# DMA transposes through DRAM for k, q, f, most of v and most head outputs

## The chip, the cores and the metric

The kernel runs on one core of one Trainium2 chip. The metric is the time of one execution in microseconds; lower is better. The core has a matrix engine (PE, with its weight loads shown as PEld), a vector engine (DVE), a scalar engine (ACT), GpSimd (POOL), and SyncE (SP), whose queue here only issues DMAs. ACT can issue DMAs from its own queue too. Sixteen DMA engines carry what these queues issue.

## The reference

Two layers of a decoder trunk over 256 tokens of width 2048, in float32. Each layer normalises h, multiplies it by one wide input matrix (8208 columns), and gives the columns to two groups of heads: group A, eight heads of gated DeltaNet in chunkwise form (short causal conv and SiLU on q, k, v, l2-normed q and k, a triangular inverse), and group B, eight heads of HGRN2 (a gated linear recurrence). Each head's output is RMS-normed and gated, the outputs are joined and multiplied by an output matrix; then a per-layer embedding gated by a sigmoid is added.

```python
for l in range(DEPTH):
    hn = rms_norm(h, norm_w[l])
    proj = hn @ w_in[l]
    dn_qkv, dn_z, dn_b, dn_a, hg_q, hg_f, hg_i, hg_z = jnp.split(proj, split_points, axis=-1)
    y_a = deltanet_branch(dn_qkv, dn_z, dn_b, dn_a, ...)
    y_b = hgrn2_branch(hg_q, hg_f, hg_i, hg_z, lower_bounds[l], hg_norm_w[l])
    h = h + jnp.concatenate([y_a, y_b], axis=-1) @ w_out[l]
    gate = jax.nn.sigmoid(h @ w_ple_gate[l])
    h = h + (p[l] @ w_ple_up[l]) * gate
return rms_norm(h, final_norm_w)
```

## The kernel before, in words

**Dense products.** Weights arrive from DRAM in float32 and are split into two parts whose product PE takes at its fast float32r rate: `whi`, a rounded copy made by ACT (L438), and `wlo`, the remainder made by DVE (L440). Activations are split in the same way (`split`: hi on ACT, lo on DVE). Each product is three matmuls (hi x hi, lo x hi, hi x lo), all recorded at L377. The work of a layer is a list of steps: a step is two row blocks (128 each) of the weights for 512 columns, 12 matmuls; a chunk of columns is 8 such steps. Chunks 0 (z of the first group and the two gate inputs, 272 columns) and 10 (v of the first group alone, 256 columns) take four row blocks in a step. The input stage has 17 chunks in the order of `in_order()`: z and gates, kq of groups 0 to 3, then fq(0), iz(0), fq(1), iz(1), fq(2), v(0), vz(1), iz(2), vz(2), fq(3), vz(3), iz(3). A "group" is two heads. The out stage and the gate stage have four chunks of 512 columns each; the first two chunks of each stage are interleaved.

**Loads.** `ahead(n)` is called before step n: it issues loads (L419, SP's queue, three buffers `raw`) and makes the splits two steps ahead (three buffers `whi` and `wlo`).

**The work between.** All the rest (conv, gates, inverse, states, norms) is written as generators. `spawn` starts one; each `yield n` hands back the number of steps that it wants to wait, and `tick()`, called after each step, advances those whose count has run out. A generator that yields a function waits until that is true. The numbers come from the tables `DELAY` (by kind of work: d DeltaNet, i inverse, b the turning of h, h HGRN2) and `DELAY_AT` (by group or layer, as "d2yp"). PE's order is the program's order; `while not pairs_ready(...)` in the out and gate stages calls `tick()` with no step between when an operand isn't made yet.

**Transposes.** The projection gives tokens on partitions, the mixers want channels on partitions. `evict` copies a chunk from PSUM to SBUF on ACT (tile `et`); `turned` turns it on PE in groups of four 128x128 transposes (L380) into PSUM. This is done for k and q (`dkdq`), f and q of HGRN2 (`hfhq`), v (`dv`, which is turned a second time after conv and SiLU: tile `pv`), and each head output (`head_norm`: tile `yt`, turned into `yp`, then split to `y[kp]`; kp is 0 to 3 for DeltaNet's groups, 4 to 7 for HGRN2's). The out stage takes its row blocks in the order of `OUT_KTS`, so it wants y[4], y[5], y[0], y[1], y[6], y[2], y[3], y[7]:

```python
OUT_KTS = (8, 9, 10, 11, 0, 1, 2, 3, 12, 13, 4, 5, 6, 7, 14, 15)
```

For three of four chunks of h, before the gate stage (g) and before the next layer (n), the turn already goes by DMA (`turn_by_dma`): ACT copies 16-bit halves apart (L548), a DMA transpose on SP's queue goes from SBUF to SBUF (L551), and ACT joins the halves again (L556).

**The inverse.** When the fourth group has given its matrix (`given`, a write to DRAM from ACT's queue, L682), `Inverse.run` makes the triangular inverse of all groups in a chain of DVE and PE work, with DMAs through DRAM. v of a group then goes through pz, pS, pw, pz, po to its output.

Of the kernel before, what the change touches and what calls it, by code (L numbers as in the profile page):

```python
# [8 lines left out]
F32 = mybir.dt.float32  # L9
# [24 lines left out]
def chunk_cols(chunk):  # L34
# [3 lines left out]


DELAY = {  # L40
    "d": {'c': 1, 'D': 4, 'k': 6, 'q': 7, 'ssq': 1, 'v': 5, 'z0': 1, 'S': 1, 'w': 1, 'z1': 1, 'o': 1, 'y': 3, 'yp': 1},
    "i": {'F': 4, 'F2': 1, 'F3': 1, 'F4': 1, 'w': 2, 'b': 1, 'T': 2, 't16': 3, 'p16': 2, 't32': 3, 'p32': 2, 't64': 3, 'p64': 2},
    "b": {'o': 1, 'g': 4},
    "h": {'c': 1, 'f': 1, 'x2': 1, 'x4': 1, 'x8': 1, 'a': 2, 'x16': 1, 'x32': 1, 'x64': 1, 'u16': 2, 'u64': 1, 'o': 2, 'y': 2, 'yp': 1, 'q': 0},
}

DELAY_AT = {
# [14 lines left out]
}  # L62


XB = 1, 1, 4, 1, 1


def delay(kind, g, step):
# [107 lines left out]
def trunk(ctx: ExitStack, tc: tile.TileContext, head, xT, x, pT, W, par, fw, cst, msk, eye, out):  # L176
# [311 lines left out]
    def tmp(name, shape=(128, 512)):  # L488
        return tp.tile([128, 512], F32, tag="tmp", name=name)

    def sigmoid(dst, src, e=None):

        if e is None:
            S.activation(dst, src, AF.Exp, scale=-1.0)
            V.tensor_scalar(dst, dst, BIG, 1.0, ALU.min, ALU.add)
        else:
            S.activation(e, src, AF.Exp, scale=-1.0)
            V.tensor_scalar(e, e, BIG, None, ALU.min)
            V.tensor_scalar(dst, e, 1.0, None, ALU.add)
        S.activation(dst, dst, AF.Ln)  # L500
        S.activation(dst, dst, AF.Exp, scale=-1.0)

# [27 lines left out]
    def turn(c, name, scales):  # L530
# [8 lines left out]
            out.append(split(ps, 2 * c + half, scales(2 * c + half), name))  # L539
        return out  # L540

    def turn_by_dma(c, name, scales):

        u16 = lambda ap: ap.bitcast(U16)
        flat, across = (u16(mix("et", 1024, 2, f"{name}{x}{c}")).rearrange("p (w k m b) -> p w k m b", w=2, k=4, m=2)
                        for x in "pq")
        for m in range(2):
            S.copy(flat[:, :, :, m], u16(h[c][:, m]).rearrange("p (k b w) -> p w k b", k=4, w=2))  # L548
            yield XB[m]
        every = lambda ap: ap.rearrange("p w k m b -> p (w k m) b")  # L550
        nc.sync.dma_start_transpose(every(across), flat.rearrange("p w k m b -> p (w k m b)"))  # L551
        yield XB[2]
        out = []
        for half in range(2):
            t = tmp(f"{name}t{c}{half}")
            S.copy(u16(t).rearrange("p (b w) -> p w b", w=2),  # L556
                   across[:, :, 2 * half:2 * half + 2].rearrange("p w k m b -> p w (k m b)"))
            yield XB[3 + half]
            out.append(split(t, 2 * c + half, scales(2 * c + half), name))
        return out  # L560

    first_ss = []
# [51 lines left out]
    def mix(tag, n, bufs, name):  # L614
        return mp.tile([128, n], F32, tag=tag, name=name, bufs=bufs)
# [4 lines left out]
    def head_norm(o, f, sz, nw, kp, y, name, wait):  # L620

        yt = tmp(name + "yt")
        for i in range(4):
            hh, t = divmod(i, 2)
            V.scalar_tensor_tensor(v4(yt)[:, i], o[:, i], f[:, i:i + 1],
                                   sz[:, 256 * t + 128 * hh:256 * t + 128 * hh + 128], ALU.mult, ALU.mult)
        yield wait
        ps = pm.tile([128, 512], F32, tag="m", name=name + "yp")
        for i in range(4):
            PE.transpose(ps[:, 128 * i:128 * i + 128], v4(yt)[:, i], ident)  # L630
        y[kp] = split(ps, kp, [nw], name)

    def gate_z(ps, c0, rt, name):
# [6 lines left out]
        G.tensor_tensor(sz, zs, sz, ALU.mult)  # L640
        return sz

    def evict(ps, c0, n, rt, name):

        et = mix("et", 1024, 2, name + "et")[:, :2 * n].rearrange("p (t n) -> p t n", t=2)
        for t in range(2):
            S.activation(et[:, t], ps[t][:, c0:c0 + n], AF.Copy, scale=rt[:, t:t + 1])
        return et

    def turned(et, c0, name):  # L650

# [10 lines left out]
    class Inverse:  # L662
# [2 lines left out]
        NT = 4 * NG  # L665

        def __init__(self, l):
            self.n, self.l, self.Bt, self.have, self.ready = f"di{l}", l, None, 0, False

        def wait(self, step):  # L670
            return delay("i", self.l, step)
# [122 lines left out]
    class DN:  # L794
# [41 lines left out]
        def conv(self, ps, which):  # L836
# [11 lines left out]
            sg = tmp(n + "sg")  # L848
            sigmoid(sg, ac)
            return ac, sg  # L850

        def conv_silu_kq(self, ps, which, w):
            ac, sg = self.conv(ps, which)
            for t in range(2):
                V.tensor_tensor(self.kq[t][:, :, w, :], v4(ac)[:, t::2], v4(sg)[:, t::2], ALU.mult)

# [10 lines left out]

        def dkdq(self, ps, c0):
            n = self.n
            et = evict(ps, c0, 512, self.row.rt, n + "kq")  # L870
            yield self.wait("c")
            pk, pq = turned(et, 0, n + "pkc"), turned(et, 256, n + "pqc")
            self.kq = [mix(f"kq{t}", 512, 2 + 2 * t, n + f"kq{t}").rearrange("p (h w c) -> p h w c", h=2, w=2)
                       for t in range(2)]
            self.conv_silu_kq(pk, 1, 0)
            spawn(self.k_side())
            self.conv_silu_kq(pq, 0, 1)
            spawn(self.q_side())

        def k_side(self):  # L880
# [52 lines left out]

        def dv(self, ps, c0):
            n, kq, g = self.n, self.kq, self.g
            et = evict(ps, c0, 256, self.row.rt, n + "v")
            yield self.wait("c")
            ac, sg = self.conv(turned(et, 0, n + "pvc"), 2)
            V.tensor_tensor(ac, ac, sg, ALU.mult)
            yield self.wait("v")  # L940
            yield self.after("b")
            pv = pm.tile([128, 512], F32, tag="m", name=n + "pv")
            for i in range(4):
                PE.transpose(pv[:, 128 * i:128 * i + 128], ac[:, 128 * i:128 * i + 128], ident)
# [35 lines left out]
            po = pm.tile([128, 512], F32, tag="m", name=n + "po")  # L980
            for i in range(4):
                PE.matmul(po[:, 128 * i:128 * i + 128], self.QK[:, i], v1[:, i], start=True, stop=True)
            o = v4(tmp(n + "o"))
            S.copy(o[:, 0::2], v4(po)[:, 0::2])
            V.tensor_tensor(o[:, 1::2], v4(po)[:, 1::2], qs, ALU.add)
# [9 lines left out]
            yield from head_norm(o, f, self.sz, P("dnw", self.l), g, self.y, n, self.wait("yp"))  # L995

    class HG:

# [16 lines left out]
            yield 1  # L1015

        def hfhq(self, ps, c0):
            et = evict(ps, c0, 512, self.row.rt, self.n + "fq")
            yield self.wait("c")
            spawn(self.f_side(turned(et, 0, self.n + "pf")))  # L1020
            spawn(self.q_side(turned(et, 256, self.n + "pq")))

        def f_side(self, fs):
            l, g, n = self.l, self.g, self.n
            e, sg = tmp(n + "fe"), tmp(n + "fsg")
            sigmoid(sg, fs, e)
# [13 lines left out]
        def q_side(self, qr):  # L1040
# [5 lines left out]
            sigmoid(sg, qr)  # L1046
# [133 lines left out]
        def hz(self, ps, c0):  # L1180
            g = self.g
            sz = gate_z(ps, c0, self.row.rt, self.n)
            yield self.wait("y")
            yield self.after("o")
            yield from head_norm(self.o, self.f, sz, P("hnw", self.l), 4 + g, self.y, self.n, self.wait("yp"))


    def banks(name, c):
# [293 lines left out]
```

## Time and profile before

| | |
|---|---|
| Median of 3 runs | 1234.73 us (1233.22 to 1235.4) |
| The profiled execution's own time | 1233.27 us |
| Its span, first to last instruction | 1231.6 us |
| Granted clock of PE | 0.998 |
| Busy: PE, DVE, ACT | 1216.1, 880.9, 807.7 us |
| DMA queue of the loads, share of 16 engines | 54.7% |

"Busy" is the time in which an engine had an instruction under way. The chain that ended last is followed back from the last instruction: at each step to what released it, or to the instruction before it on its engine. A row of a tile's view gives count, the durations (least, median, most, in ns), and when the first and the last started. In a view of waits the numbers are the total in us, how many times, and the longest. Names like dn02pkc are tiles: dn or hg, the layer, the group, the tile.

### The profile page before, as it was taken

Reading aid. Unit: us, or ns where it says so; the run is one execution under the profiler, and the core shown is the slowest. Engines: PE = TensorE matmul, PEld = TensorE weight load, DVE = VectorE, ACT = ScalarE, POOL = GpSimd, SP = SyncE. Lnnn points to the kernel's source line nnn. Section 1 sums busy time; section 2 is a strip of 40 time slices with the busy share of each in tenths; the row PEclk is TensorE's granted clock in tenths of the full one; section 3 lists DMA queues with packets and bytes.
Section 4 is the critical chain, followed back from the end, with each engine's and each line's share of the span. In section 5 each row is a group of like instructions: output and inputs, shape, how many; then the busy total and the mean of one; then the engine's idle time right before and its main releaser. Section 6 shows DMA issues by size and latency. Waiting matters only on the chain.

```text
span 1231.6 us, 21477 instructions
## 1 busy us (share of the span) xinstructions
PE 1216.1 (99%) x8282; PEld 1021.8 (83%) x8282; DVE 880.9 (72%) x1537; ACT 807.7 (66%) x1376; POOL 75.3 (6%) x67
## 2 busy tenths in 40 slices
PE   9999999999999999999999999999999999999997
PEld 8888887898888888888888888878888888888886
DVE  7777897887568756547668879877875696565565
ACT  7676766586757757548866667674857676575453
POOL 0310000000000100000003100000000010000020
PEclk9999999999999999999999999999999999999999
DMA  8555455534464456657665555555444555686564
GB/s 290 177 193 175 159 182 164 188 139 170 156 213 150 171 176 210 219 197 202 222 188 177 180 175 175 174 176 159 132 147 150 175 159 178 199 214 222 180 205 137
DMA packets 92727, 223.42 MB, mean 181 GB/s; under 512 B 34256, under 2 KB 39760, under 8 KB 92624
## 3 DMA queue, kind: packets, MB, share of 16 engines
q1 hardware_dynamic: 82400, 216.65, 54.7%
q10 hardware_dynamic: 10224, 5.39, 1.6%
q8 instruction: 65, 1.06, 0.3%
q14 instruction: 38, 0.31, 0.1%
HBM read 212.84 MB, written 4.46 MB: 176 GB/s over the span
## 4 chain that ended last, share of the span: by engine, by line
PE 93%; ACT 4%; issue 1%; DMA 1%; DVE 1%; POOLq 0%; POOL 0%; ACTq 0%; DVEq 0%
PE out L377 14%; PE gate L377 11%; PE in0hf L377 7%; PE in1hf L377 7%; PE in1dk L377 7%; PE in1hi L377 7%; PE in0hi L377 7%; PE in0dv L377 6%; PE in1dv L377 6%; PE in0dk L377 5%; PE up L377 1%; ACT whi L438 1%; PE in0dz L377 1%; PE in1dz L377 1%; DMA n1q<-n1p 0%
## 5 line engine op out<-in xcount | busy, mean ns | idle before, releaser
L440 DVE TENSOR_TENSOR wlo<-raw,whi 128x1024 fp32r<-128x1024 f32 (+2 forms) x393 | 479.6, 1224 | 278.3 <-ACT whi L438 273.0
L438 ACT ACTIVATE whi<-raw 128x1024 fp32r<-128x1024 f32 (+2 forms) x393 | 408.9, 1045 | 249.6 <-PE gate L377 51.1
L377 PE MATMUL in1hi<-whi,n1hi 128*128 128x512 f32 x128 | 41.0, 402 | 0.0
L377 PE MATMUL in1hf<-whi,n1hi 128*128 128x512 f32 x128 | 40.5, 398 | 0.0
L377 PE MATMUL in1dk<-whi,n1hi 128*128 128x512 f32 x128 | 40.4, 397 | 0.0
L377 PE MATMUL gate<-whi,g0hi 128*128 128x512 f32 x128 | 39.6, 391 | 0.2 <-ACT pg L1236 0.2
L377 PE MATMUL in1hi<-whi,n1lo 128*128 128x512 f32 x128 | 39.7, 391 | 0.0
L377 PE MATMUL in1dk<-whi,n1lo 128*128 128x512 f32 x128 | 39.6, 390 | 0.0
L377 PE MATMUL in1hf<-whi,n1lo 128*128 128x512 f32 x128 | 39.5, 390 | 0.0
L377 PE MATMUL gate<-whi,g0lo 128*128 128x512 f32 x128 | 39.4, 389 | 0.0
L377 PE MATMUL in1dv<-whi,n1hi 128*128 128x512 f32 (+1 forms) x128 | 36.5, 376 | 0.0
L377 PE MATMUL gate<-whi,g1hi 128*128 128x512 f32 (+1 forms) x120 | 35.7, 379 | 0.0
L377 PE MATMUL gate<-whi,g1lo 128*128 128x512 f32 (+1 forms) x120 | 35.7, 379 | 0.0
L377 PE MATMUL in1dk<-wlo,n1hi 128*128 128x512 f32 x128 | 35.6, 390 | 0.0
L377 PE MATMUL in1hi<-wlo,n1hi 128*128 128x512 f32 x128 | 35.6, 390 | 0.0
L377 PE MATMUL in1hf<-wlo,n1hi 128*128 128x512 f32 x128 | 35.6, 389 | 0.0
L377 PE MATMUL gate<-wlo,g0hi 128*128 128x512 f32 x128 | 35.5, 389 | 0.0
L377 PE MATMUL in1dv<-whi,n1lo 128*128 128x512 f32 (+1 forms) x128 | 34.9, 364 | 0.0
L377 PE MATMUL gate<-wlo,g1hi 128*128 128x512 f32 (+1 forms) x120 | 32.4, 379 | 0.0
L377 PE MATMUL in1dv<-wlo,n1hi 128*128 128x512 f32 (+1 forms) x128 | 31.5, 363 | 0.0
L377 PE MATMUL in0hi<-whi,n0hi 128*128 128x512 f32 x96 | 30.8, 402 | 0.0
L377 PE MATMUL in0hf<-whi,n0hi 128*128 128x512 f32 x96 | 30.7, 401 | 0.0
(1491 smaller groups left out, 2917.1 us busy)
## 6 DMA issues: line engine op xcount, KB each, us to landing
raw<-W SPq DMA_DIRECT2D x383, 512.0 KB, 3.6
raw<-W SPq DMA_DIRECT2D x7, 544.0 KB, 3.9
h<-x SPq DMA_DIRECT2D x4, 512.0 KB, 4.9
xt<-xT SPq DMA_DIRECT2D x3, 512.0 KB, 6.6
out_dram<-h SPq DMA_DIRECT2D x5, 256.0 KB, 2.3
di0d<-di0Bt ACTq DMA_DIRECT2D x4, 256.0 KB, 2.4
di1d<-di1Bt ACTq DMA_DIRECT2D x4, 256.0 KB, 2.3
fw<-fw ACTq DMA_DIRECT2D x2, 512.0 KB, 4.0
```

The costliest lines, as they stand in the source:

```text
L377: return tc.keep_in_program_order(nc.tensor.matmul(*a, **k))
L438: S.activation(hi[:, sl], raw[:, sl], AF.Copy)
L440: V.tensor_tensor(lo[:, sl], raw[:, sl], hi[:, sl].bitcast(F32), ALU.subtract)
```

## The change

The transposes of k and q, of f and q (all groups), of v in groups 0 to 2 (both turns), and of head outputs 0, 1, 2, 4, 5 go by DMA. `apart` copies the 16-bit halves of each word apart on ACT, one copy per 128 tokens and a step ahead of each, and writes them to DRAM from ACT's queue. `across` issues a DMA transpose from DRAM to SBUF on SP's queue; since the two halves of a word are neighbouring rows in DRAM, the words come back whole. `turn_by_dma` uses the same two functions, and so loses the copy that joined the halves. The group 3 of v and the outputs 3, 6, 7 stay on PE. The sigmoids are cut into steps (`sigmoid_in_steps`), the conv into taps and SiLU with steps between, and a group of v starts its state steps only when the group before has finished its own (`inv.through`). The distances are set anew.

```diff
-    "d": {'c': 1, 'D': 4, 'k': 6, 'q': 7, 'ssq': 1, 'v': 5, ... 'y': 3, 'yp': 1},
+    "d": {'c': 3, 'D': 4, 'k': 6, 'q': 7, 'ssq': 1, 'v': 5, 'z0': 1, 'S': 1, 'w': 1, 'z1': 1, 'o': 1, 'y': 3, 'yp': 1, 'e': 2, 've': 2, 'vc': 3, 'vp': 1, 'vt': 2, 'vq': 3, 'ye': 2, 'yt': 3, 's': 1, 's1': 1, 's2': 1},
-    "b": {'o': 1, 'g': 4},
+    "b": {'o': 1, 'g': 4, 'e': 2, 't': 3},
-    "h": {'c': 1, ...
+    "h": {'c': 3, ... 'e': 2, 'ye': 2, 'yt': 3, 's2': 1},
...
-    "d1k": 5, "d1ssq": 3, "d1w": 2, "d1y": 4, "d1yp": 2,
-    "d2D": 3, "d2k": 9, "d2o": 4, "d2q": 11, "d2ssq": 4, "d2v": 6, "d2yp": 2,
+    "d1D": 6, "d1c": 5, "d1e": 4, "d1k": 5, "d1ssq": 3, "d1vt": 3, "d1w": 2, "d1y": 2, "d1yp": 2, "d1yt": 4,
+    "d2D": 6, "d2k": 9, "d2o": 4, "d2q": 11, "d2s2": 2, "d2ssq": 4, "d2v": 4, "d2yt": 4,
...
-XB = 1, 1, 4, 1, 1
+V_DMA = 0, 1, 2
+Y_DMA = 0, 1, 2, 4, 5
...
+    def apart(src, name, into=None):
+        n, c = src.shape[1:]
+        for t in range(n):
+            yield 1
+            if not t:
+                flat = (tmp if n * c == 512 else et_tile)(name + "pl") if into is None else into
+                flat = u16(flat).rearrange("p (n w c) -> p n w c", n=n, w=2)
+            S.copy(flat[:, t], u16(src[:, t]).rearrange("p (c w) -> p w c", w=2))
+        d = dr.tile([256 * n * c], U16, tag=f"tr{n * c}", name=name + "d", bufs=4)
+        nc.scalar.dma_start(out=d.rearrange("(n p x) -> p n x", n=n, p=128), in_=flat.rearrange("p n w c -> p n (w c)"))
+        return d, c, n * c
+
+    def across(x, name):
+        d, c, f = x
+        t = (tmp if f == 512 else et_tile)(name + "tr")
+        nc.sync.dma_start_transpose(u16(t).rearrange("p (k r) -> p k r", k=c // 128), d.rearrange("(r c) -> r c", c=c))
+        return t
...
-        yield wait
-        ps = pm.tile([128, 512], F32, tag="m", name=name + "yp")
-        for i in range(4):
-            PE.transpose(ps[:, 128 * i:128 * i + 128], v4(yt)[:, i], ident)
+        if kp in Y_DMA:
+            x = yield from apart(yt.unsqueeze(1), name + "yp")
+            yield wait("ye")
+            ps = across(x, name + "yp")
+            yield wait("yt")
+        else:
+            ...
         y[kp] = split(ps, kp, [nw], name)
...
         def dkdq(self, ps, c0):
-            et = evict(ps, c0, 512, self.row.rt, n + "kq")
+            x = yield from apart(evict(ps, c0, 512, self.row.rt, n + "kq")[0], n + "kq")
+            yield self.wait("e")
+            t = across(x, n + "kq")
             yield self.wait("c")
-            pk, pq = turned(et, 0, n + "pkc"), turned(et, 256, n + "pqc")
+            pk, pq = t[:, 0:512], t[:, 512:1024]
...
+            ak = self.taps(pk, 1)
+            yield self.wait("s")
+            aq = self.taps(pq, 0)
+            yield self.wait("s1")
+            yield from self.silu_kq(ak, 0)
             spawn(self.k_side())
+            yield self.wait("s1")
+            yield from self.silu_kq(aq, 1)
             spawn(self.q_side())
...
         def dv(self, ps, c0):
+            if g in V_DMA:
+                x = yield from apart(et, n + "v", e[:, 512:1024])
+                yield self.wait("ve")
+                t = across(x, n + "v")
+                yield self.wait("vc")
+            ...
+            ac, sg = self.taps(t, 2), tmp(n + "sg")
+            yield self.wait("s1")
+            yield from sigmoid_in_steps(sg, ac, self.wait("s2"))
             V.tensor_tensor(ac, ac, sg, ALU.mult)
+            if g in V_DMA:
+                x = yield from apart(ac.unsqueeze(1), n + "pv")
+                yield self.wait("vt")
+                pv = across(x, n + "pv")
+                yield self.wait("vq")
+                yield self.after("b")
+            ...
-            yield lambda: self.inv.ready
+            yield lambda: self.inv.ready and self.inv.through == g
...
         def hfhq(self, ps, c0):
-            et = evict(ps, c0, 512, self.row.rt, self.n + "fq")
+            x = yield from apart(evict(ps, c0, 512, self.row.rt, self.n + "fq")[0], self.n + "fq")
+            yield self.wait("e")
+            t = across(x, self.n + "fq")
             yield self.wait("c")
-            spawn(self.f_side(turned(et, 0, self.n + "pf")))
-            spawn(self.q_side(turned(et, 256, self.n + "pq")))
+            spawn(self.f_side(t[:, 0:512]))
+            spawn(self.q_side(t[:, 512:1024]))
```

More of the change, by code (lines that the diff above doesn't have):

```diff
@@ L489, in tmp, with sigmoid, sigmoid_in_steps @@
         return tp.tile([128, 512], F32, tag="tmp", name=name)
-    def sigmoid(dst, src, e=None):
+    def sigmoid(dst, src):
+        for r in sigmoid_in_steps(dst, src, None):
+            pass
+    def sigmoid_in_steps(dst, src, w, e=None):
         if e is None:
@@ L499, in sigmoid @@
             V.tensor_scalar(dst, e, 1.0, None, ALU.add)
+        yield w
         S.activation(dst, dst, AF.Ln)
@@ L540, in turn @@
         return out
-    def turn_by_dma(c, name, scales):
[L544 to L552, printed above, removed]
+    u16 = lambda ap: ap.bitcast(U16)
+    def apart(src, name, into=None):
[14 more added lines that the diff above has]
+        return t
+    def turn_by_dma(c, name, scales):
+        x = yield from apart(h[c], f"{name}{c}")
+        yield delay("b", c, "e")
+        t = across(x, f"{name}{c}")
+        yield delay("b", c, "t")
         out = []
         for half in range(2):
[L555 to L559, printed above, removed]
+            out.append(split(t[:, 512 * half:512 * half + 512], 2 * c + half, scales(2 * c + half), name))
+            if not half:
+                yield 1
         return out
@@ L626, in head_norm @@
                                    sz[:, 256 * t + 128 * hh:256 * t + 128 * hh + 128], ALU.mult, ALU.mult)
-        yield wait
-        ps = pm.tile([128, 512], F32, tag="m", name=name + "yp")
-        for i in range(4):
-            PE.transpose(ps[:, 128 * i:128 * i + 128], v4(yt)[:, i], ident)
+        if kp in Y_DMA:
[4 more added lines that the diff above has]
+        else:
+            yield wait("yp")
+            ps = pm.tile([128, 512], F32, tag="m", name=name + "yp")
+            for i in range(4):
+                PE.transpose(ps[:, 128 * i:128 * i + 128], v4(yt)[:, i], ident)
         y[kp] = split(ps, kp, [nw], name)
@@ L641, in gate_z, with et_tile @@
         return sz
+    def et_tile(name):
+        return mix("et", 1024, 2, name)
     def evict(ps, c0, n, rt, name):
-        et = mix("et", 1024, 2, name + "et")[:, :2 * n].rearrange("p (t n) -> p t n", t=2)
+        e = et_tile(name + "et")
+        et = e[:, :2 * n].rearrange("p (t n) -> p t n", t=2)
         for t in range(2):
             S.activation(et[:, t], ps[t][:, c0:c0 + n], AF.Copy, scale=rt[:, t:t + 1])
-        return et
+        return et, e
     def turned(et, c0, name):
@@ L667, in __init__ @@
         def __init__(self, l):
-            self.n, self.l, self.Bt, self.have, self.ready = f"di{l}", l, None, 0, False
+            self.n, self.l, self.Bt, self.have, self.ready, self.through = f"di{l}", l, None, 0, False, 0
         def wait(self, step):
@@ L834, in decay, with taps @@
             self.done.add("D")
-        def conv(self, ps, which):
+        def taps(self, ps, which):
             l, g, n = self.l, self.g, self.n + "qkv"[which]
@@ L847, in conv, with silu_kq @@
                     V.scalar_tensor_tensor(a, ps[:, 256 * m:256 * m + 253 + j], P("cw", w0(m) + j), a, ALU.mult, ALU.add)
[L848 to L853, printed above, removed]
+            return ac
+        def silu_kq(self, ac, w):
+            sg = tmp(f"{self.n}sg{w}")
+            yield from sigmoid_in_steps(sg, ac, self.wait("s2"))
             for t in range(2):
@@ L935, in dv @@
             n, kq, g = self.n, self.kq, self.g
-            et = evict(ps, c0, 256, self.row.rt, n + "v")
-            yield self.wait("c")
-            ac, sg = self.conv(turned(et, 0, n + "pvc"), 2)
-            V.tensor_tensor(ac, ac, sg, ALU.mult)
[L940 to L944, printed above, removed]
+            et, e = evict(ps, c0, 256, self.row.rt, n + "v")
+            if g in V_DMA:
[3 more added lines that the diff above has]
+                yield self.wait("vc")
+            else:
+                yield self.wait("vp")
+                t = turned(et, 0, n + "pvc")
+            ac, sg = self.taps(t, 2), tmp(n + "sg")
+            yield self.wait("s1")
+            yield from sigmoid_in_steps(sg, ac, self.wait("s2"))
+            V.tensor_tensor(ac, ac, sg, ALU.mult)
+            if g in V_DMA:
[4 more added lines that the diff above has]
+                yield self.after("b")
+            else:
+                yield self.wait("v")
+                yield self.after("b")
+                pv = pm.tile([128, 512], F32, tag="m", name=n + "pv")
+                for i in range(4):
+                    PE.transpose(pv[:, 128 * i:128 * i + 128], ac[:, 128 * i:128 * i + 128], ident)
             R = v4(mix("R", 512, 2, n + "R"))
             V.tensor_tensor(R, v4(pv), bc(self.invn, 128), ALU.mult)
-            yield lambda: self.inv.ready
+            yield lambda: self.inv.ready and self.inv.through == g
             yield self.wait("z0")
@@ L982, in dv @@
                 PE.matmul(po[:, 128 * i:128 * i + 128], self.QK[:, i], v1[:, i], start=True, stop=True)
+            self.inv.through += 1
             o = v4(tmp(n + "o"))
@@ L994, in dv @@
             yield self.after("z")
-            yield from head_norm(o, f, self.sz, P("dnw", self.l), g, self.y, n, self.wait("yp"))
+            yield from head_norm(o, f, self.sz, P("dnw", self.l), g, self.y, n, self.wait)
     class HG:
@@ L1025, in f_side @@
             e, sg = tmp(n + "fe"), tmp(n + "fsg")
-            sigmoid(sg, fs, e)
+            yield from sigmoid_in_steps(sg, fs, self.wait("s2"), e)
             self.k = mix("hk", 512, 1, n + "k")
@@ L1045, in q_side @@
             sg = tmp(n + "qsg")
-            sigmoid(sg, qr)
+            yield from sigmoid_in_steps(sg, qr, self.wait("s2"))
             c32 = lambda ap: ap.rearrange("p (a c) -> p a c", c=32)
@@ L1184, in hz @@
             yield self.after("o")
-            yield from head_norm(self.o, self.f, sz, P("hnw", self.l), 4 + g, self.y, self.n, self.wait("yp"))
+            yield from head_norm(self.o, self.f, sz, P("hnw", self.l), 4 + g, self.y, self.n, self.wait)
     def banks(name, c):
```

4 lines of the change are left out of this document (removed), and 21 rows, old and new, of tables (DELAY, DELAY_AT).

## The prediction

> **What bounds the kernel now.** I read the page first: its busy parts, the queues, the chain that ended last, the costliest groups.
>
> ```profile
> span 1231.6 us, 21477 instructions
> PE 1216.1 (99%) x8282; PEld 1021.8 (83%) x8282; DVE 880.9 (72%) x1537; ACT 807.7 (66%) x1376; POOL 75.3 (6%) x67
> q1 hardware_dynamic: 82400, 216.65, 54.7%
> PE 93%; ACT 4%; issue 1%; DMA 1%; DVE 1%; POOLq 0%; POOL 0%; ACTq 0%; DVEq 0%
> L440 DVE TENSOR_TENSOR wlo<-raw,whi 128x1024 fp32r<-128x1024 f32 (+2 forms) x393 | 479.6, 1224 | 278.3 <-ACT whi L438 273.0
> L438 ACT ACTIVATE whi<-raw 128x1024 fp32r<-128x1024 f32 (+2 forms) x393 | 408.9, 1045 | 249.6 <-PE gate L377 51.1
> raw<-W SPq DMA_DIRECT2D x383, 512.0 KB, 3.6
> ```
>
> PE is busy for 1216.1 of 1231.6 us and holds 93% of the chain; no other engine is near. So PE work that goes comes off the end, as long as nothing new makes PE wait. Next the waits: PE's own, and those of the weight path (loaded by SP, split by ACT and DVE).
>
> ```profile
> PE hg11pa L377 <- issue: 2.2, 1, 2.2
> PE hg00yp L380 <- DVE hg00yt L625: 1.3, 1, 1.3
> PE hg10yp L380 <- DVE hg10yt L625: 1.3, 1, 1.3
> PE dn00pg L377 <- DVE dn00kq L855: 0.6, 1, 0.6
> ACT whi L438 <- DMA raw<-W: 28.0, 20, 2.9
> SPq L419 <- DVE wlo L440: 706.0, 275, 7.4
> ```
>
> Inside the span PE waits for a few us only. SP's queue stands 706.0 us waiting for a raw buffer to come free, so it has room. Then the chain in order of time, for what a transpose costs PE:
>
> ```profile
> 92.82 2.76 PE in0dk L377 x12
> 95.57 0.44 PE dn02pkc L380 x4
> 96.01 0.44 PE dn02pqc L380 x4
> 203.53 1.02 PE hg00yp L380 x4
> 263.83 0.44 PE dn00pvc L380 x4
> 278.72 0.44 PE hg01yp L380 x4
> ```
>
> A step of 12 dense matmuls takes 2.76 us; all distances in the table count such steps. A group of four transposes takes 0.44 us of PE, whichever tile it turns; only hg00yp, which had to wait for its input, holds 1.02.
>
> **What PE loses.** Per layer: k and q of four head groups are 8 groups of four transposes, f and q likewise 8, v of three head groups, turned twice, 6, and the head outputs 0, 1, 2, 4, 5 are 5. That is 27, in two layers 54: 54 x 0.44 = 23.8 us. Head output 4 (hg00yp, hg10yp) waits no more in PE's order: 2 x (1.3 + 1.02 - 0.44) = 3.8 us. The 0.6 us before dn00pg goes as well: the conv of k and q gets steps of its own, and the 6 steps of "d0q" start only when q is made. Together 28.2 us.
>
> **What ACT gets.** Each path now takes copies of halves and the issue of a write on ACT, and a transpose issued on SP. The nearest rows are those of the paths that already go by DMA, and of the DRAM write of Bt:
>
> ```profile
> L548 ACT COPY g0p<-h 128x1024 uint16<-128x1024 uint16 x6 | 6.1, 1040 | 4.8 <-DVE h L1222 3.8 <-DMA g0q<-g0p 0.9
> L556 ACT COPY n1t<-n1q 128x1024 uint16<-128x1024 uint16 x6 | 7.8, 1350 | 1.6 <-DMA n1q<-n1p 1.6
> L682 ACTq DMA_DIRECT2D di0d<-di0Bt x4: 366/372/389, 67.8 to 154.3; - x4
> DMA to landing us min/median/max: 2.3/2.5/4.7
> L551 SPq DMA_TRANSPOSE g0q<-g0p x3: 1427/1757/3087, 467.8 to 495.9; - x3
> L551 SPq DMA_TRANSPOSE n1q<-n1p x3: 3419/3471/3855, 564.7 to 599.2; - x3
> DMA to landing us min/median/max: 4.3/5.2/5.9
> ```
>
> (The first landing is that of the Bt writes, the second that of the transposes.) Per layer in the input stage: 16 copies of 1.04 for kq and fq, 6 of half that size for v (0.52), 3 for the second turn of v and 5 for the outputs (1.04): 28 us, and 19 issues of 0.37: 7 us. The whole-word return takes 18 copies of 1.35 (24 us) out of the out and gate stages, where they cost PE nothing. Is there room for 35 us per layer?
>
> ```profile
> core 0: us, PE busy (x) PEld busy (x) DVE busy (x) ACT busy (x) POOL busy (x), PEclk, DMA share, GB/s
> 0.00:422.00 422.00, 418.86 (x3253) 352.21 (x3253) 330.43 (x652) 290.38 (x542) 30.86 (x34) 1.00 0.54 181
> 614.00:1031.00 417.00, 413.56 (x3244) 349.01 (x3243) 321.95 (x611) 280.99 (x516) 28.34 (x19) 1.00 0.54 168
> 260.00:280.00 20.00, 20.00 (x170) 16.82 (x164) 19.45 (x43) 17.30 (x38) 0.00 (x0) 1.00 0.36 128
> 560.00:580.00 20.00, 20.00 (x90) 16.55 (x89) 13.96 (x18) 20.00 (x32) 0.00 (x0) 1.00 0.71 210
> ```
>
> ACT rises from 290 of 422 us (69%) to 325 of about 408 (80%), DVE stands at 330 of 408 (81%). The last two rows say what such a load does: DVE at 19.45 with ACT at 17.30 of 20 us, or ACT at 20.00 of 20, and PE lost nothing. I cost it at nothing by these two; if that cover is gone, see the second rival.
>
> **What SP gets.** 19 new transposes per layer (8 of 512 KB, 11 of 256 KB), queued among the loads, and a wait for the DRAM write ahead of each; behind it stands the next load, and for that wait the split on ACT, then PE. The slack of a load: three raw buffers last 3 x 2.76 = 8.3 us, less the split (1.05 + 1.22) and a landing of 3.6, leaves 2.4; the split is made two steps ahead, 5.5 - 2.3 = 3.2 more: 5.6 us until PE stands. Against it, with the worst of the rows: copy 1.04, issue 0.39 and write 4.7 are 6.1 us, and the two steps between write and transpose cover 5.5, so 0.6 of wait, and 3.9 of issue: 4.5 us. A transpose alone is hidden. Counting the distances, transposes come bunched about three times a layer (those of v of the first two groups with head output 5; of dn0's output, fq of the fourth group and v of the third; the inverse's eight small DMAs with that of head output 4). Two back to back take 2 x 3.9 of issue and 0.6 of wait, 8.4 us, and come 2.8 us late; say 3 us six times, 18 us. The ends are 0 and 18 us; no end below nothing, since it adds work to a queue. I take 3 us, near the lower, because most bunched ones are of 256 KB and six of nine issues shown took 1.4 to 3.1.
>
> The consumers wait 3 to 5 steps (8 to 14 us) after the transpose is issued, against a landing of up to 5.9: covered, if a DRAM source lands like the SBUF source of the rows. That is not shown. DMA load grows: per layer 8 x (0.5 + 0.5) and 11 x (0.25 + 0.25) MB, and 9 writes of 0.5 for g and n, some 32 MB beside 217; 54.7% of the engines becomes about 63%, and the window with 0.71 shows PE unhurt. At the weighing of DMA against PE a rule speaks against the change: the Trainium skill, page "VectorE: DVE Perf Modes", section "Rules for kernel authors", says to transpose 128x128 on TensorE if PSUM will do as destination, and its section "The three transpose paths" gives 1309 ns for a DMA turn of one 2-byte block. By that price, blocks one after the other, the 16 blocks of a kq tile would take 21 us (an estimate from that page) and each of the 16 large ones would come 10 us late, a sum near 1365 us; the rows have 5.9 us at most for a tile of this size, so they do not bear that out.
>
> **The steps anew.** The chain of a layer gets longer: from the end of chunk (dv2, dz2) to the output of group 2, the distances sum to 20 steps before (1+6+1+1+1+1+4+3+2) and to 34 after (2+2+3 to the conv, 1+2 in the sigmoid, 1+2+3 to R, 1+1+1+1+4 to o, 3, 1+2+4 for the output). The first use is step 33: two chunks of 8 and the 8 of (hi3, hz3), then the tenth step of the out stage. So one tick there runs without work between, and the split of that output ends right before PE wants it:
>
> ```profile
> L521 ACT ACTIVATE dn03hi<-dn03yp,pr x1: 689/689/689, 457.3 to 457.3; 128x512 fp32r<-128x512 f32 x1
> L524 DVE SCALAR_TENSOR_TENSOR dn03lo<-dn03yp,pr,dn03hi x1: 745/745/745, 458.1 to 458.1; 128x512 fp32r<-128x512 f32 x1
> ```
>
> If both are exposed it costs 1.4 us a layer, 2.8 us; the ends are 0 (ACT and DVE run ahead of PE) and 2.8, and I take 2.8. The outputs of groups 3 and 7 stay on PE, one and two steps ahead of their use. Elsewhere the distances of the inverse and the state steps stay as they were, only later.
>
> **The sum.** Against the profiled execution (span 1231.6, run 1233.27): - 28.2 + 3 + 2.8 = - 22.4, so 1210.9; the median of the runs, 1234.73, lies 1.46 above that run, which makes 1212.3. I say 1212.
>
> **The rivals.** *The DRAM transpose is slow (slower).* Place: SP's queue, the load behind each transpose. Every transpose shown reads SBUF; none shows issue or landing from DRAM. It decides once each of the 38 comes 28.2/38 = 0.74 us later than the slack allows; at 1.5 us each it is 57 - 28 = 29 us slower: 1263. For it: n1q's issue took twice g0q's at the same size, so the issue is not a fixed price. Against: SP's 706 us of room. The Trainium skill's rule above would come out on this side, with the price given there; I give it 0.02 of this rival's chance, as the rows of 5.9 us speak against it. *ACT and DVE fall behind in the input stage.* DVE waits 273.0 us for ACT's split, in order; adding 35 us per layer to ACT in stretches where it has 17.3 of 20 could cost some 3 us in each of the four fullest stretches: 12 us lost, 1224. *Nothing moves.* The transposes go, but bunched loads (18 us) and late outputs, a second tick's worth at each layer's end (2 x 2.8), take back 24 to 28: 1233. Against: PE's few waits show a weight path with slack.
>
> **How the numbers follow.** My forecast, with its unknowns from all hidden and the 2.2 us of issue at hg11pa gone too (1234.7 - 30.4 = 1204) to 1219: 0.70. ACT and DVE behind, 1219 to 1230: 0.15. Nothing moves: 0.05. Slower by the DRAM transpose: 0.10. The range 1204 to 1228 holds 0.70 and most of the 0.15. A change within 0.2% (2.5 us) is what a measurement cannot tell from none; faster 0.85, same 0.05, slower 0.10.
>
> **What would show it.** Right: 432 instructions fewer on PE (216 matmuls and their loads), PE's busy time near 1192, hg00yp gone from PE's waits, ACT in the input stage near 80%, few us under waits of PE for the weight splits. Wrong: PE waiting for wlo or whi, ACT waiting for raw far above 28 us, transposes on SP that take over 4 us to issue or 10 to land, or PE standing before the tenth step of the out stage for more than 3 us.

## The result and the profile after

The changed kernel takes 1244.03 us (median of 6 runs, 1239.78 to 1248.58), the kernel before, beside it, 1235.07 us: a ratio of 1.0078, 95% interval 1.0051 to 1.0105. It is slower; the prediction said 1212. The profiled execution after has a span of 1242.6 us. Its page, in the order of the lines shown of before:

```profile
span 1242.6 us, 21219 instructions
PE 1203.8 (97%) x8066; PEld 1002.4 (81%) x8066; DVE 877.7 (71%) x1537; ACT 829.5 (67%) x1418; POOL 81.7 (7%) x67
...
q1 hardware_dynamic: 138912, 230.81, 60.2%
q10 hardware_dynamic: 20960, 24.27, 6.0%
...
PE 74%; DMA 8%; DVE 7%; ACT 6%; issue 3%; SPq 1%; ACTq 0%; POOLq 0%; POOL 0%; DVEq 0%
...
raw<-W SPq DMA_DIRECT2D x383, 512.0 KB, 4.0
```

The work went as announced: 216 matmuls fewer, PE's busy time down by 12.3 us. But PE's share of the chain fell from 93% to 74%; DMA, DVE, ACT and "issue" hold the rest. The waits, as sum, count and longest, first PE's largest, then ACT's and SP's:

```profile
PE hg02pa L378 <- issue: 5.1, 1, 5.1
PE hg01pa L378 <- issue: 3.0, 1, 3.0
PE in0hi L378 <- ACT dn03zs L665: 3.0, 1, 3.0
PE in1dk L378 <- ACT dn12kqet L679: 2.3, 1, 2.3
PE in0hf L378 <- ACT dn03kqet L679: 1.8, 1, 1.8
ACT whi L439 <- DMA raw<-W: 55.5, 47, 5.4
SPq L568 <- DMA dn02kqd<-dn02kqpl: 6.3, 1, 6.3
SPq L568 <- DMA dn10pvd<-dn10pvpl: 6.1, 1, 6.1
```

All rows of PE together are 30.2 us (6.7 before). Three things are new or larger. In the rows that name kqet, fqet, vet and zs, PE starts a chunk of the input stage and its PSUM bank has not been evicted yet: ACT is late with the eviction (about 17 us over all). For the weight splits (whi) PE waits 2.3 us only. In the "issue" rows PE waits for nothing the profile shows. And ACT waits twice as long for loads (55.5 us for 28.0), while SP stands at L568, the DMA transpose, until the write ahead of it has landed: 34 such waits, 94.6 us (8 of them, 15.0 us, at the turns of h).

One tile shows how it goes. The timeline of ACT and of SP around it (start, duration, instruction, and the idle time before it):

```profile
93.08 1.05 ACT L559 COPY dn02kqpl<-dn02kqet 128x1024 uint16<-128x1024 uint16 x1
...
94.17 0.38 ACTq L561 DMA_DIRECT2D dn02kqd<-dn02kqpl  x1
...
101.22 1.33 SPq L568 DMA_TRANSPOSE dn02kqtr<-dn02kqd  x1
102.64 1.03 SPq L420 DMA_DIRECT2D raw<-W  x2
...
105.61 0.51 ACT L875 ACTIVATE dn02kac<-dn02kqtr,pr 128x256 f32<-128x256 f32 x1 [6.07 <-DMA dn02kqtr<-dn02kqd]
```

The write is issued at 94.17 and lands 7.0 us later. SP, which waits 6.3 us, was there at 94.9, 0.7 us after the write's issue and not two steps (5.5 us) after it. The two loads queued behind it go at 102.64, back to back, and ACT, in order, stands 6.07 us until the transposed tile is there. PE's wait for the eviction of a bank comes later (from the chain in order of time, start and duration):

```profile
394.83 5.75 DMA dn02pvtr<-dn02pvd
...
400.61 0.07 DVE dn02R L1000
...
401.67 0.63 ACT hg03qsg L507
...
403.35 0.36 ACT dn03vet L679
...
405.05 0.37 ACT dn03zs L665
405.46 2.27 PE in0hi L378 x6
```

This is the chain of waits at a chunk's end: a DVE instruction has waited for a turned tile to land, a sigmoid on ACT comes late behind it, the last eviction, dn03zs, follows the sigmoid, and PE's next chunk starts 0.04 us after it. Last, the granted clock, in windows (the columns as in the prediction):

```profile
280.00:300.00 20.00, 18.11 (x354) 14.87 (x355) 16.93 (x38) 16.57 (x36) 1.28 (x1) 0.91 0.47 151
300.00:320.00 20.00, 14.87 (x166) 11.97 (x155) 11.38 (x30) 8.80 (x15) 0.00 (x0) 0.83 0.71 193
...
400.00:420.00 20.00, 17.00 (x80) 14.15 (x79) 18.63 (x36) 16.00 (x28) 1.47 (x1) 0.91 0.48 154
```

With each of PE's three longest stands (2.97 us from 278.92, 5.13 from 300.48, 3.00 from 402.46) the clock went to one half for a while: 3.4, 6.8 and 3.4 us from 283.4, 303.8 and 406.2 on. That is 6.8 us of PE lost, less 0.9 in which PE still stood: some 6 us.

### The profile page after: what moved, and what is told of

It is laid out like the page before. It is cut to its first block, busy times and chain, and to the rows that moved or that the text cites. A ratio compares the mean times of both kernels' runs of the same rounds, so it can differ in the third digit from the quotient of the medians.

```text
span 1242.6 us, 21219 instructions
## 1 busy us (share of the span) xinstructions
PE 1203.8 (97%) x8066; PEld 1002.4 (81%) x8066; DVE 877.7 (71%) x1537; ACT 829.5 (67%) x1418; POOL 81.7 (7%) x67
## 4 chain that ended last, share of the span: by engine, by line
PE 74%; DMA 8%; DVE 7%; ACT 6%; issue 3%; SPq 1%; ACTq 0%; POOLq 0%; POOL 0%; DVEq 0%
PE out L378 14%; PE gate L378 13%; PE in1hi L378 6%; PE in1dk L378 5%; PE in0hi L378 5%; PE in0dv L378 5%; PE in1hf L378 5%; PE in1dv L378 4%; DMA raw<-W 3%; PE in0dk L378 3%; DVE wlo L441 3%; ACT whi L439 3%; PE in0hf L378 2%; PE up L378 2%; SPq L568 1%
## 5 line engine op out<-in xcount | busy, mean ns | idle before, releaser
L439 ACT ACTIVATE whi<-raw 128x1024 fp32r<-128x1024 f32 (+2 forms) x393 | 409.1, 1045 | 238.9 <-DMA raw<-W 55.5
```

The source lines that it names most:

```text
L439: S.activation(hi[:, sl], raw[:, sl], AF.Copy)
```

## The experiments

Ratios are to the kernel before, run on the same chip, with their 95% intervals; 0.001 is 1.24 us. Unless said otherwise an edit is to the changed kernel. "Unread" means that the work behind takes the tile as it was ahead of the turn, so that values which should be turned are not.

**Where it lies.** The first kernel keeps ACT's copies of halves and leaves out the new writes and transposes; its following work reads the unturned tile. The second issues all DMAs, unread.

```
 def apart(...):                       # e1_no_dma, dn and hg tiles
+    return src, c, n * c              # behind the copies: no write
 def across(x, name):                  # no transpose: the tile itself
+    return d.rearrange("p n c -> p (n c)")
 # e2_dma_unread: the write and the transpose stay, then
+    return src.rearrange("p n c -> p (n c)")
```

> The changed kernel without the DMA part of the new paths: for k, q, f, v and the head outputs the copies of halves on ACT stay, but nothing is written to DRAM or transposed, and what follows reads the tile that was not turned (the turning is left out, so the numbers computed are others). Theory 1 (the round trip through DRAM is longer than the distances, so ACT stands in order at tiles that have not landed, and evictions at the ends of chunks come late): about 1212, PE waiting under 6 us, no wait of PE on evictions above 1 us. Theory 2 (not the DMAs but ACT's additional copies and the new cut of the sigmoids put late work ahead of evictions): stays above 1235, with the same waits on evictions. Theory 3 (the traffic delays PE's instruction fetch and the weight loads): about 1215, with the waits named issue back to 2 us.

> The changed kernel with all writes and transposes issued as they are, but what follows reads the tile that was not turned, so nobody waits for a landing except the transpose for its write (the turning is left out of the result). Theory 1: most of the loss goes, 1212 to 1220. Theory 2: above 1235. Theory 3: 1228 to 1240, the issue waits of 3 and 5 us and late loads (ACT waiting for raw near 55 us) stay.

Measured: 1218.44 us without the DMAs, 0.9853 (0.9834 to 0.9872); 1248.94 us unread, 1.0101 (1.0082 to 1.0120). In the kernel without the DMAs PE waits for evictions 1.8 us in all; of its waits:

```profile
PE hg01pa L378 <- issue: 4.0, 1, 4.0
PE hg02pa L378 <- issue: 3.6, 1, 3.6
PE in0dk L378 <- ACT dn01kqet L683: 0.9, 1, 0.9
```

So ACT's copies and the order of its work cost PE nothing worth mention; the DMA part costs 0.0225, 28 us, and that does not come from work that stands at a tile not yet landed, since without readers it is not faster. The same time only moves from tiles to loads. Of the unread kernel:

```profile
ACT whi L439 <- DMA raw<-W: 85.9, 55, 5.6
PE in0dk L378 <- ACT dn02kqet L681: 2.4, 1, 2.4
PE in0dv L378 <- DVE wlo L441: 2.6, 1, 2.6
```

**Parts put back on TensorE.** v and pv; the head outputs; k, q, f.

```
-V_DMA = 0, 1, 2                       # e3_v_on_pe
+V_DMA = ()
-Y_DMA = 0, 1, 2, 4, 5                 # e4_y_on_pe
+Y_DMA = ()
-    x = yield from apart(...); yield self.wait("e"); t = across(...); yield self.wait("c")
+    yield 2 + self.wait("e") + self.wait("c")      # e8_kqf_on_pe
+    pk, pq = turned(et, 0, ...), turned(et, 256, ...)
```

> The changed kernel with v of all groups back on PE (48 transposes more, 12 groups of four: + 5.3 us of PE). Theory 1: the waits at late v tiles go (some 6 us with what follows): 1240 to 1245. Theory 3: the bunch of three writes near 298 us goes, and with it the issue wait of 5.1 us and its slow clock: 1233 to 1238. Theory 2: 1245 to 1250.

> The changed kernel with all head outputs back on PE (40 transposes more, 10 groups of four: + 4.4 us of PE, and the two waits before hg00yp and hg10yp may return, + 3.8). Theory 1: ACT's waits of 4 us at the tiles of head output 4 go, but they come away from chunk ends: 1243 to 1250. Theory 3: one write of the bunch near 298 us goes, the issue wait shrinks: 1238 to 1243. Theory 2: 1248 or more.

> The sixteen tiles of k with q and of f with q (512 KB each) are turned on TensorE again, at the step at which their transposed tile was read; v, pv and the head outputs keep their DMA transposes. TensorE gets back 32 of the 54 groups of four transposes (32 x 0.44 = 14 us), SP loses 16 of 38 new transposes (their issue, about 41 us of the 72, and their waits for writes). Theory that SP's queue carries the loss (17 us for issue with traffic, 11 for waits): about half to two thirds of 28 us goes with these sixteen, so 1244 + 14 - 16 = about 1242, between 1236 and 1246. Theory that the 256 KB pieces carry it (their waits for writes were the longest): 1244 + 14 - 9 = about 1249. With v or the head outputs alone put back the time was 1252 and 1249; if each part put back costs the same way, 1255.

Measured: e3 1252.5 us, 1.0128 (1.0110 to 1.0147); e4 1249.34 us, 1.0102 (1.0081 to 1.0123); e8 1252.03 us, 1.0124 (1.0097 to 1.0151). None is faster than the whole change. But each gives PE work back, by the estimate of 0.44 us per group 5.3, 4.4 and 14 us, and is only 6, 3 and 6 us slower than the whole change. So of the 28 us e3 takes nothing away, e4 about 1, and e8, with 16 of the 38 tiles, about 8 (by the intervals, each to some 4 or 5 us): together 9. The parts do not add up to the whole, and the loss belongs to no one kind of tile. With only the 22 pieces of 256 KB left (e8), PE still waits at chunk ends, now for the gates:

```profile
PE in1hi L378 <- ACT dn13zs L665: 4.8, 1, 4.8
PE in0dv L378 <- ACT hg02zs L665: 3.7, 1, 3.7
```

Why e8 gives back no more, with ACT's waits for loads at 46.4 us for 55.5, is not settled.

**Waits for the writes and the place of the transpose.** e5 is the unread kernel with transposes that read a fixed part of the weights. e10 issues each transpose one step later. e7 writes each copy by itself. e9 keeps the writes and leaves the new transposes out, unread.

```
+        d = u16(W[0:128 * f])                       # e5_no_write_wait
+    return d + (step in ("e", "ve", "vt", "ye")) - (step in ("c", "t", "vc", "vq", "yt"))   # e10_one_step_later
+            nc.scalar.dma_start(... [:, t], in_=flat[:, t] ...)    # e7_halves, per copy
+        return src.rearrange("p n c -> p (n c)")    # e9_writes_only, ahead of the transpose
```

> As the run in which nobody reads the transposed tile (1248.9), but the 38 new transposes read a fixed part of the weights in DRAM, so SP does not wait for the write ahead of each; the writes are still made, and the number and size of all DMAs stay (the turning is left out of the result). Theory 4 (SP stands 95 us in 34 waits for writes, and the loads behind come late): falls to 1222 to 1232, ACT's wait for raw from 86 back to some 40 us. Theory 3 (the traffic itself): stays at 1240 to 1248.

> Every transpose is issued one step later and its reader waits one step less, so the reader stands where it stood. If the waits for the writes are what delays the loads (94.6 us in 34 waits, 2.8 us each, one step is about 2.75 us): the sum of these waits falls to about 25 us, the time by up to 11 us to about 1234 (1231 to 1239). If the transposes' arrival is the limit, the readers come too early and the time rises to 1247 or more. If only issue and traffic count: 1244 as it was.

> The changed kernel with each copy written to DRAM by its own DMA, so the first half leaves a step earlier and the transpose waits for 256 KB or 128 KB only; 11 more issues a layer on ACT. Theory 4: SP's waits for writes shrink by a third or more, 1236 to 1240. Theory 3: unchanged within 2 us or slower by the 8 us of issue spread over ACT.

> The writes of the new paths stay, their transposes are left out, and what follows reads the tile that was not turned. Theory 4: close to the run without DMA, 1218 to 1224. Theory 3, if writes are the part that contends: 1230 or more; if transposes are: 1218 to 1222.

Measured: e5 1237.81 us, 1.0018 (1.0001 to 1.0034); e10 1255.80 us, 1.0145 (1.0120 to 1.0169); e7 1253.64 us, 1.0138 (1.0115 to 1.0161); e9 1220.72 us, 0.9871 (0.9857 to 0.9886). The writes cost nothing that can be told from e1. e5 took away less than meant: SP's waits for writes fell from 95.9 to 63.3 us, because the 512 KB tiles still wait for the buffer that the write reads. Even so it is 0.0083, 10 us, faster than the unread kernel, though ACT's waits for loads stayed (84.5 us for 85.9); whether a part of that is the other source of its transposes, no run tells. e7 left most of the waits (88.4 us in 27) and is 7 us slower than the whole change. e10 hardly changed the waits (81.3 us in 30): from a write's issue to SP's arrival at its transpose the median is 2.9 us, with one step fewer 2.6. The reason is in SP's queue: counted in loads, 28 of the 38 new transposes stand behind the same load in e10 as in the changed kernel, since the order of the queue is not the program's count of steps alone. So e10 does not tell what one step more between a write and its transpose is worth. What sets SP's arrival is the load ahead of the transpose. For dn03kq the write is issued at 120.88; DVE's split, which frees a buffer, ends at 123.07; that load is out at 123.43, and SP stands at the transpose, 2.54 us after the write's issue.

**No wait for a write, but readers.** The transposes read the halves of the group before and land in the tile just copied; or plain reads do.

```
+    d, before[key] = before.get(key, d), d          # e11_transposes_no_wait
+    nc.sync.dma_start_transpose(u16(src...), d...)
+    nc.sync.dma_start(out=src..., in_=W[0:128 * f]...)    # e12_plain_reads
```

> Writes stay. The new transposes are issued where they were, with the same sizes, but read the halves that the group before wrote, and put them into the tile that the copies have just read (no wait for a write, none for a free buffer); the work behind reads them, so the values are those of another group. Against the kernel with the writes alone (1220.7) it adds the issue of 38 transposes on SP (72 us) and 15 MB of transposed traffic, without waits. If issue and traffic cost 17 us by themselves: about 1237. If the waits that were left in the kernel without waits for the small writes (63 us, for the writes of the 512 KB tiles through their buffers) carried that: about 1224.

> As the kernel before it in this list, but each new transpose is a plain read of as many bytes from the weights into the same tile: the traffic stays, 38 x 0.33 us of issue instead of 38 x 1.9. If the time on SP's queue carries the loss: within 3 us of the kernel with the writes alone, 1220.7 to 1224. If the traffic carries it: as with the transposes, about 1237.

Measured: 1261.94 us, 1.0210 (1.0188 to 1.0233); 1247.30 us, 1.0081 (1.0057 to 1.0104). Both expectations were missed, and the waits of SP say why. Of e11:

```profile
SPq L573 <- ACT whi L439: 38.7, 11, 6.6
SPq L573 <- ACT lq L977: 19.0, 3, 7.5
```

Here SP waits for ACT, 97.4 us in 28, because the tile may not be overwritten until ACT has copied it (60.6 us in 30 with plain reads). The copy lies two steps or more ahead of the transpose in the program, and SP is there first all the same. The two kernels do not take the waits away; what they show is the difference between transposes and plain reads of as many bytes at the same places, 0.0129 or 16 us.

**Each cost by itself, on top of the writes.** SP issues, in place of the transpose: plain reads that depend on nothing (e15); small transposes that depend on nothing (e18); a 16 KB read of what was written (e17); one or two 16 KB transposes of it (e19); a plain copy of all of it to DRAM (e20).

```
+    nc.sync.dma_start(out=scratch, in_=W[0:128 * f]...)            # e15_reads_alone
+    for j in range(f // 512):                                      # e18_issue_alone
+        nc.sync.dma_start_transpose(t, u16(W[0:64 * 64])...)
+    nc.sync.dma_start(out=t, in_=d...[:, :64])                     # e17_waits_alone
+    for j in range(f // 512):                                      # e19_waits_and_issue
+        nc.sync.dma_start_transpose(t, d[8192 * j:8192 * j + 8192]...)
+    nc.sync.dma_start(out=scratch, in_=d...)                       # e20_waits_and_reads
```

> The writes stay; in place of each new transpose SP issues a plain read of as many bytes from the weights into a scratch place in DRAM, which waits for nothing and for which nobody waits. Traffic alone, then, and 38 x 0.33 us on SP's queue. If the traffic carries the loss: 1235 or more. If not: 1220 to 1224, as with the writes alone (1220.7).

> The writes stay; in place of each new transpose of 256 KB SP issues one DMA transpose of 16 KB of the weights, and two in place of one of 512 KB, which wait for no write and for which nobody waits: issue time of about 54 x 1.2 = 65 us on SP's queue (72 in the changed kernel), with next to no traffic. If the issue carries the loss: about 1235. If the waits carry it: 1221 to 1225.

> The writes stay; in place of each new transpose SP issues a small plain read (16 KB) of what the write leaves, so that it waits for the write as before, with almost no issue time and no traffic; nobody reads it. If SP's waits for the writes carry the loss (94.6 us in 34 waits): 1232 or more. If issue or traffic carry it: 1221 to 1225.

> As the kernel with the waits alone (1223.5), but what SP issues behind each wait is a DMA transpose of 16 KB of what the write left, one for a tile of 256 KB and two for one of 512 KB: 54 x 1.2 = 65 us of issue (72 in the changed kernel), at the place where the changed kernel has it, next to no traffic, nobody reads the result. If the issue behind the wait carries the loss: 1240 to 1249, near the kernel whose transposed tiles nobody reads (1249). If the traffic of the transposes carries it: 1224 to 1229.

> As the kernel with the waits alone, but what SP issues behind each wait is a plain copy of all that the write left to another place in DRAM (512 or 256 KB): the waits and the traffic, 0.4 us of issue each, nobody reads the result. If the traffic carries the loss: 1240 to 1249. If the issue does: 1224 to 1230.

Measured: e15 1226.99 us, 0.9937 (0.9922 to 0.9952); e18 1253.95 us, 1.0153 (1.0136 to 1.0170). In both, the DMAs, which wait for nothing, had been moved by the program's scheduler into the span's first 135 us. Of e18, SP's timeline and PE's longest wait:

```profile
99.72 1.68 SPq L570 DMA_TRANSPOSE dn10yptr<-W  x1
101.44 0.58 SPq L420 DMA_DIRECT2D raw<-W  x1
102.12 1.09 SPq L570 DMA_TRANSPOSE dn11yptr<-W  x1
```

```profile
PE in0dk L378 <- ACT whi L439: 15.6, 6, 9.6
```

Tiles of the second layer, whose transposes stood at 976 and 996 after, go near 100. So these two do not price the places of the change; e18 shows only that a crowd of transposes between the loads starves PE (15.6 us). Those that read what was written stayed in place: e17 1223.54 us, 0.9912 (0.9897 to 0.9927); e19 1231.16 us, 0.9969 (0.9943 to 0.9996); e20 1227.70 us, 0.9930 (0.9907 to 0.9953). In microseconds, by the ratios: the waits alone (89.4 us on SP; at the same paths of the changed kernel 79.6) cost 5; the issue behind them 7 more than that; a plain copy behind them 2 more, which cannot be told from nothing; the whole transposes, unread, 23 more. So the three parts give 14 of the 28 us that lie between e9 and the unread transposes. ACT's wait for loads grows with them. With the writes alone:

```profile
ACT whi L439 <- DMA raw<-W: 37.4, 31, 3.6
```

with the waits, and with waits and issue:

```profile
ACT whi L439 <- DMA raw<-W: 50.3, 45, 3.0
```

```profile
ACT whi L439 <- DMA raw<-W: 77.2, 53, 5.6
```

and 71.6 with waits and copies, 85.9 with the unread transposes. These waits are no measure of the cost: 71.6 us goes with 7 us over e9, 77.2 with 12. The traffic of a transpose is heavier than that of a copy of as many bytes. The loads' queue on three pages (packets, MB, share of 16 engines), with the writes alone, with the copies and with the unread transposes:

```profile
q1 hardware_dynamic: 82400, 216.65, 56.5%
q1 hardware_dynamic: 83616, 230.81, 59.1%
q1 hardware_dynamic: 138912, 230.81, 61.2%
```

Times their spans (1218.2, 1225.8 and 1247.2 us) that is 688, 724 and 763 us: 36 more for the copies, 75 for the transposes. Whether the other 14 us of the kernel's time are this traffic, or the three parts together once ACT's lead is used up, no run here separates; e5, where a third of the waits was worth 10 us beside the transposes and all of them 5 without, says that the parts do not simply add. The 16 us between e11 and e12 speak for the traffic, less the 7 of issue, but e11 also waited longer for ACT.

**Loads in a queue of their own.**

```
-        i = nc.sync.dma_start(out=raw[:, :f]          # e16_loads_on_gpsimd
+        i = (nc.gpsimd if n > 17 else nc.sync).dma_start(out=raw[:, :f]
```

> The changed kernel, with the loads of the weights on GpSimd's queue (GpSimd is busy for 7% of the span) and the transposes and their waits alone on SP's. If the loads come late because they stand behind the transposes: the wait of ScalarE for loads falls from 55 us to about 30, the time to between 1218 and 1230. If the traffic or the arrival of the tiles carries the loss: 1240 to 1250. A third case: GpSimd issues a load more slowly than SP or holds it behind its own work, and the time rises above 1250.

Measured: 1346.16 us, 1.0869 (1.0812 to 1.0927), the third case. Of its page, and of its waits:

```profile
PE 1240.1 (92%) x8066; PEld 1021.4 (76%) x8066; DVE 880.5 (65%) x1537; ACT 828.0 (61%) x1418; POOL 273.6 (20%) x441
...
raw<-W POOLq DMA_DIRECT2D x370, 512.0 KB, 4.4
```

```profile
ACT whi L439 <- DMA raw<-W: 110.3, 62, 6.3
```

POOL is busy for 192 us more with 374 loads, 0.5 us each, and the loads come later still. With loads this late the run does not tell whether the transposes would cost nothing beside a queue of their own.

**The "issue" waits.** In the chain the small matmuls of the inverse (di0pp) run straight into those of hg02pa, and then PE stands:

```profile
298.06 1.13 PE di0pp L378 x64
299.19 1.29 PE hg02pa L378 x99
300.48 5.13 issue
305.61 0.30 PE hg02pa L378 x6
```

e6 moves one step of the inverse by one step:

```
-    "i0t16": 5
+    "i0t16": 6                        # e6_inverse_apart
```

> The changed kernel with the inverse of layer 0 one step later after its first transposes (i0t16 6 for 5), so that its 64-matmul bursts no longer stand in the same step as those of hg01 and hg02. Theory 5 (the issue waits and the half clock behind them come from two bursts of small matmuls back to back, not from DMA): the waits of 3 and 5 us and 10 us of half clock go, 1244 - 13 = 1231. Theory 3 (DMA traffic holds up the fetch): 1240 to 1244.

Measured: 1245.77 us, 1.0077 (1.0056 to 1.0098), no gain, though the rows with "issue" are gone (9.0 us after). Two others took their place:

```profile
PE in0dv L378 <- ACT hg02zs L665: 5.7, 1, 5.7
PE in0hi L378 <- ACT dn03zs L665: 4.7, 1, 4.7
```

So the wait goes when the two bursts are apart, but taking it away only lets PE reach the next late eviction sooner. It is not the work of the new DMAs, since e1 has it too. Bursts side by side are not enough for it: in the kernel before, 64 small matmuls of di0px (1.98 us from 281.86) run into 128 of hg02pa (1.39 us), and PE does not stand. Why it stands is open.

## Why the prediction was wrong

**What PE loses** (-28.2). The groups went (busy time fell by 12.3 us, although some 6 us of it are lost to the clock; in e1 it fell by 24.0 without the clock's part, for 23.8 in the sum), and so did the waits at hg00yp and hg10yp. But the kernel without DMAs is 18 us faster (0.0147), where the sum without the SP term has 25.4, and 28.2 without the late outputs, which were not seen either (below). In e1 the "issue" waits are 7.6 us for 2.2 before, and its clock stands at one half for 10.2 us, which costs some 5: 28.2 - 5.4 - 5 is 18. The new distances put bursts of small matmuls side by side, and the clock falls with the stands. The prediction looked at neither.

**What ACT gets** (0). Held as far as the load goes: e1 has all the copies and loses next to nothing to evictions. The second rival was right about where PE would stand and wrong about why: ACT is late since it has stood for a load or a tile (without the DMAs the late evictions are gone), and busy for 16.57 of 20 us, as from 280 us on, it has little to win the time back with; this last is argued and not tested. That a chunk's eviction has only about 1.4 us of slack, six matmuls (an estimate: half a step of 2.76 us, while PE fills the other bank), was overlooked, and so the two quiet windows proved less than was drawn from them.

**What SP gets** (+3): the step that failed. It said that the two steps between write and transpose cover 5.5 us, so 0.6 us of wait is left. The waits are 2.8 us in the mean and 6.3 at most. Of its parts, the landing of a write was 4.5 us in the median and 10.3 at most (2.5 and 4.7 in the rows of Bt that it took), and the issue of all 47 transposes takes 95.3 us of SP (23.5 before for 9), 2.0 us for each and less than the 3.9 that it reckoned with. The deeper fault is that a count of steps was read as time between engines. SP arrives at a transpose 2.6 us after the write's issue, by the median, as soon as a split has given a buffer to the load ahead of it, and in e11 it is there ahead of ACT's copy. The path was another too: the sum let PE stand for the splits of late loads, and there PE waits 2.3 us; late loads and tiles hold ACT, in order, and PE stands about 17 us for ACT's evictions. The term is 26 to 28 us in place of 3 (the changed kernel less e9, and less e1), which alone turns the sum to slower: put on the writes one by one, the waits give 5 of it and the issue 7, and how the larger half comes about stays open.

**Consumers and the steps anew.** The landing of a transpose from DRAM, not shown when the prediction was made, is 4.5 us in the median and 7.9 at most, for 5.2 and 5.9 before. Readers do stand (6.07 us above), yet the unread kernel is no faster, so that is not a cost of its own. The late outputs (+2.8) were not paid: no wait of PE in the out stage stands among its rows.

**The rivals.** The first, a slow DRAM transpose with its place at the load behind it, comes nearest: right in place and sign, too dear with 1263, since not each of the 38 exceeds the slack. Its reason does not hold, since the transposes are not slow: 2.0 us of issue in the mean, for 2.6 before. "Nothing moves" had the bunched loads as its reason and 24 to 28 us as its price; the price was right by luck, with 5.6 us of late outputs in it, and the issue waits and the clock put the time above it. The marks of a wrong forecast, ACT's wait for raw far above 28 us and a transpose that takes over 4 us to issue (4.9), were both met.

## What to carry to other kernels

A distance in program order is not a distance in time: for each DMA that waits for another engine's work, read from the trace how far ahead the issuing queue runs of that engine and behind which load the DMA really stands, and count the loads behind it as late by the difference. When a helper engine is some 80% busy, look for its hard dates (the bank that PE needs next) and not for its mean load. And after moving work, look at what small matmuls now stand side by side.

## What was not expected of the hardware

- Some 160 small matmuls in 2.4 us (64 of di0pp, 99 of hg02pa) are followed by 5.13 us in which PE stands, in the middle of hg02pa, and waits for nothing that the profile shows; 145 in 2.15 us by 2.97 us. With one step between them it is gone.
- A stand of 2.97 us was followed by a granted clock of one half, for 3.4 us; in e6 one of 2.27 us too, while one of 2.29 us in the changed kernel (from 708.49) was not. The Trainium skill, page "TensorE: Matmul & The Clock Gate", section "Part 1: The HAM clock gate (the "warmup" mystery)", speaks of windows of about 3.4 us, and of at least one idle window ahead of the fall. The lengths here, 3.4 and 6.8 us, agree; these stands were shorter than a window.
- A write to DRAM from ACT's queue lands after 2.4 to 10.3 us. The longest is one of three that went within 2 us of each other, near 298.
